# Prologue of a hybrid layer: scaling moved to VectorE, the first pair's sums placed behind x1's pieces, the output weights copied later

## The chip, the core and the metric

The program runs on one core of a Trainium2 chip. The metric is the device time of one execution in microseconds; lower is better. The engines are TensorE (PE in the profile; PEld is its weight load), VectorE (DVE), ScalarE (ACT), GpSimd (POOL) and SyncE (SP), which issues most DMAs. Each engine works through its own list of instructions in order and waits on semaphores.

## The reference

One decoder layer over 1024 tokens of width 1024, all in float32: RMSNorm, one wide projection, a Mamba-2 branch and a forgetting-attention branch beside each other, a gated merge, an output projection and a second RMSNorm. Only its start matters here:

```python
h = _rmsnorm(x, pre_g)                       # x * rsqrt(mean(x^2) + eps) * pre_g
proj = jnp.einsum('bld,de->ble', h, w_in)    # -> z_ssm, xBC, dt, q, k, v, f, z_att, g_ssm, g_att
...
out  = merged @ w_out
return x + _rmsnorm(out, post_g)
```

## The kernel before

**Products in seven steps.** Every wide product runs as a Strassen-like scheme on 2x2 blocks: seven block products instead of eight, each on a combination of blocks. The moving side is h turned (features on partitions), cut into blocks b11, b21 (first 512 tokens) and b22 and combinations t1, t2, t3, t4 (which need the other 512 tokens). Each operand is kept as a high piece and a low piece, both float32r; the tiles are `x0h`/`x0l` (b11), `x1h`/`x1l` (b21), `x2` (-b22), `x3` (t1), `x4` (-t2), `x5` (t3) and `x6` (t4), with four slices each. ScalarE writes the high piece and VectorE subtracts it to get the low one (`put`, L1211 to L1218). Step 1 uses x0, step 2 uses x1, step 6 uses x4, step 5 uses x3, step 7 uses x5, step 4 x6 and step 3 x2. One step is 12 matmuls of 128x512 in two halves.

**Weights.** A `Pair` of projection columns has four raw weight tiles (`raw`, six buffers, loaded on SP's queue). A step's weights (`wop`) are split in the same way, ScalarE first (L349), VectorE behind it (L350). Steps 6, 5, 7 and 3 take sums of raw tiles, made by `total` (L355) and in `prepare` (L371). `Stream` runs the steps of all pairs in a fixed list; `ahead` prepares the step that is three places further on when a step begins. The list begins with step 1 of the first pair, step 1 of the second, step 2 of each, then steps 6, 5, 7, 4 and 3 of the first pair.

**The prologue.** Eight tiles of x, 128 tokens each, are loaded (`xt`, L1187). `norm_tiles` takes the sum of squares, the root and the reciprocal, and scales the tile: tiles 0 to 3 on VectorE (L1201), 4 to 7 on GpSimd (L1203). TensorE turns slices of four tiles into PSUM (`pt`, two buffers, L1208); the copy out of PSUM multiplies by the norm's weight and makes `low` (L1228 on ScalarE, L1230 on VectorE). For k = 0 to 7 that gives the slices of x0 and x1; from k = 4 on, half a step of the stream runs behind each. Then come four rounds (j = 0 to 3): the other tokens' two slices are turned and copied (`up` and `b`, L1248), eight matmuls into `df` follow, VectorE makes `th` (L1254, L1257), their pieces x3 and x4, and the differences in `low` (L1262, L1263), and half a step runs. Behind the rounds stand the pieces of x5, x6 and x2 while steps 6, 5 and 7 of the first pair run.

**Output weights.** Twelve DMAs copy w_out from the input into `wo_dram` (L1237), 256 KB each. Nothing in the prologue reads it.

**Order.** Matmuls, turns and the operations under `pin` keep the program's order; a scheduler places the others. DMAs of the SP and ACT queues are given eight counters in turn, and a DMA is issued only when the DMA before it on its counter has landed. The short-lived tiles `th`, `up`-differences, gates and outputs share four buffers (`small`, L136); the first gate that is computed (`th` of the first pair, L415) goes through a tanh (L629) and is stored from such a buffer to `gs_dram` on ScalarE's queue (L630).

## Time and profile before

| | |
|---|---|
| median of 3 runs | 1278.63 us (1276.34 to 1283.66) |
| profiled execution, whole | 1273.87 us |
| its span, first to last instruction | 1272.2 us |
| PE, DVE, ACT, POOL busy | 1246.1, 1012.9, 794.3, 319.3 us |
| first step of the stream begins | 18.19 us |
| VectorE finishes the fourth round's last piece of x4 | 48.12 us |
| `summing` (L1304), first work behind the prologue's products | 59.01 us |

The profile lists, by engine, when an instruction began and how long it took; a bracket gives the idle time of its engine in front of it and what ended that. Instructions on one engine overlap a little, so a group's time is less than its count times the time of one.

### The profile page before, as it was taken

What the parts mean: (1) busy time and instruction counts of PE and PEld (TensorE: products, weight loads), DVE (VectorE), ACT (ScalarE), POOL (GpSimd) and SP (SyncE); (2) the same over time, 40 slices, a digit from 0 to 9 for tenths busy, and PEclk for the clock granted to TensorE, in tenths of its full rate; (3) what the DMA queues carried; (4) which work ended last, traced back from release to release, by engine and by line L of the source; (5) the groups of instructions that cost most, each with busy time, mean ns of one, the idle gap of its engine ahead of it and who ended that gap; (6) DMA issues with size and microseconds to landing.
All of it is one profiled execution on the core that took longest, in us unless ns stands there. A gap on an engine that the chain in (4) does not pass through costs nothing.

```text
span 1272.2 us, 20822 instructions
## 1 busy us (share of the span) xinstructions
PE 1246.1 (98%) x6926; PEld 982.3 (77%) x6926; DVE 1012.9 (80%) x1994; ACT 794.3 (62%) x1737; POOL 319.3 (25%) x322
## 2 busy tenths in 40 slices
PE   5999999999999999999999999999999999999997
PEld 3678888888888888888887777777777777778886
DVE  7988886988888978997767676767789767886975
ACT  7745665556665765566555666666687666844753
POOL 4000440013400241115102124223112212356062
PEclk9999999999999999999999999999999999999999
DMA  8232452545436533744447576666687657766933
GB/s 300 69 120 76 146 162 88 191 152 182 138 101 215 175 127 117 219 146 140 142 149 252 162 228 212 217 214 218 232 286 263 224 184 249 249 221 199 364 110 105
DMA packets 152236, 233.56 MB, mean 184 GB/s; under 512 B 15201, under 2 KB 60737, under 8 KB 152129
## 3 DMA queue, kind: packets, MB, share of 16 engines
q1 hardware_dynamic: 136064, 196.08, 47.7%
q10 hardware_dynamic: 10560, 18.06, 3.8%
q0 software_dynamic: 5504, 18.09, 3.7%
q8 instruction: 54, 0.88, 0.3%
q14 instruction: 54, 0.43, 0.1%
HBM read 162.99 MB, written 72.34 MB: 185 GB/s over the span
## 4 chain that ended last, share of the span: by engine, by line
PE 86%; DMA 4%; DVE 4%; ACT 4%; issue 1%; SPq 0%; POOL 0%; DVEq 0%; ACTq 0%; POOLq 0%
PE pb L128 36%; PE pc L128 21%; PE pd L128 7%; PE av L128 5%; PE pt L131 5%; PE s L128 5%; PE yps L128 2%; PE st L128 1%; ACT ex L1509 1%; DMA xt<-in_x 1%; PE tr L131 1%; PE tr_v L131 1%; DMA v<-v_dram 1%; PE df L128 1%; DVE wop L350 1%
## 5 line engine op out<-in xcount | busy, mean ns | idle before, releaser
L350 DVE TENSOR_TENSOR wop<-sum,wop 128x512 fp32r<-128x512 f32 x180 | 140.2, 780 | 53.6 <-ACT wop L349 52.6
L349 ACT ACTIVATE wop<-sum 128x512 fp32r<-128x512 f32 x180 | 112.5, 626 | 109.0 <-DVE sum L355 52.4
L1509 ACT ACTIVATE ex<-ex,nm 128x512 f32<-128x512 f32 (+1 forms) x192 | 116.2, 606 | 71.9 <-DVE nm L1505 71.6
L402 ACT ACTIVATE s<-pb 128x512 f32<-128x512 f32 x144 | 85.3, 593 | 98.2 <-PE pb L128 96.2
L128 PE MATMUL pb<-x0h,wop 128*128 128x512 f32 x384 | 131.5, 399 | 0.0
L128 PE MATMUL pb<-x6h,wop 128*128 128x512 f32 x384 | 129.5, 395 | 1.3 <-ACT s L402 1.3
L128 PE MATMUL pb<-x5h,wop 128*128 128x512 f32 x384 | 130.1, 396 | 0.7 <-ACT s L402 0.7
L350 DVE TENSOR_TENSOR wop<-raw,wop 128x512 fp32r<-128x512 f32 x144 | 105.4, 733 | 31.8 <-ACT wop L349 31.5
L128 PE MATMUL pc<-x3h,wop 128*128 128x512 f32 x384 | 129.8, 396 | 0.5 <-DVE ot L419 0.4
L128 PE MATMUL pc<-x2h,wop 128*128 128x512 f32 x384 | 130.2, 397 | 0.0
L128 PE MATMUL pb<-x4h,wop 128*128 128x512 f32 x384 | 129.1, 395 | 0.0
L1505 DVE CUSTOM_DVE_ANT_0 ex<-s,fb 128x512 f32<-128x512 f32 (+1 forms) x192 | 96.8, 552 | 20.0 <-PE s L128 14.8
L349 ACT ACTIVATE wop<-raw 128x512 fp32r<-128x512 f32 x144 | 89.7, 623 | 14.7 <-PE pd L128 6.1
L128 PE MATMUL pd<-x1h,wop 128*128 128x512 f32 x288 | 96.3, 394 | 0.0
L128 PEld LDWEIGHTS pb<-x6h,wop 128*128 128x128 f32 x384 | 72.1, 188 | 18.6 <-issue 2.0
L128 PEld LDWEIGHTS pb<-x5h,wop 128*128 128x128 f32 x384 | 72.1, 188 | 18.4 <-issue 2.0
L128 PEld LDWEIGHTS pb<-x0h,wop 128*128 128x128 f32 x384 | 72.6, 189 | 17.6 <-issue 2.9
L128 PEld LDWEIGHTS pc<-x3h,wop 128*128 128x128 f32 x384 | 72.1, 188 | 17.7 <-issue 1.5
L128 PEld LDWEIGHTS pc<-x2h,wop 128*128 128x128 f32 x384 | 72.1, 188 | 17.4 <-issue 2.4
L128 PEld LDWEIGHTS pb<-x4h,wop 128*128 128x128 f32 x384 | 72.1, 188 | 16.7 <-issue 1.9
L211 POOL TENSOR_TENSOR wd<-wd 128x256 f32<-128x256 f32 x32 | 32.4, 1011 | 205.0 <-DMA wd<-in_wo 135.0
L131 PE MATMUL pt<-ident,ex 128*128 128x128 f32 x576 | 75.1, 273 | 2.0 <-ACT ex L1509 1.4
(318 smaller groups left out, 2993.6 us busy)
## 6 DMA issues: line engine op xcount, KB each, us to landing
raw<-in_wu SPq DMA_DIRECT2D x128, 256.0 KB
csb<-cs_dram SPq DMA_DIRECT2D x32, 256.0 KB
q<-q_dram SPq DMA_DIRECT2D x32, 256.0 KB
k<-k_dram SPq DMA_DIRECT2D x16, 512.0 KB
fb<-f_dram SPq DMA_DIRECT2D x16, 512.0 KB
rb<-st_dram SPq DMA_DIRECT2D x48, 128.0 KB
wd<-in_wo SPq DMA_DIRECT2D x40, 128.0 KB
xt<-in_x SPq DMA_DIRECT2D x8, 512.0 KB
```

Source lines behind the costliest of these rows:

```text
L128: return tc.keep_in_program_order(nc.tensor.matmul(*args, **kw))
L131: return tc.keep_in_program_order(nc.tensor.transpose(out_, in_, idn))
L211: pin(nc.gpsimd.tensor_tensor(t[out_], t[a_], t[b_], ALU.subtract))
L349: nc.scalar.activation(op[:, 0], src, AF.Copy)
L350: nc.vector.tensor_tensor(op[:, 1], src, op[:, 0], ALU.subtract)
L402: nc.scalar.activation(s, ps, AF.Copy)
L1505: nc.vector.tensor_tensor_reduce(o, s[e][:, 0:w], fb[hp, h][:, e, 0:w], 1.0, 3.0e38, ALU.add, ALU.min, nm)
L1509: pin(nc.scalar.activation(o, o, AF.Exp, scale=-1.0, bias=nm, accum_out=hd.at(hd.sm, i, h, e)))
```

## The change

Four things are changed, and every one lies in the prologue.

1. `norm_tiles` scales all eight tiles of x on VectorE. The four scalings of tiles 4 to 7 are placed behind the low piece of x0's last slice (`held`).
2. The copies of turned slices k = 2 and 3 are made by VectorE, as k = 0 and 1 were; ScalarE keeps k = 4 to 7.
3. The first pair's sums in `total` are placed behind the last low piece of x1 (`behind`), and `ahead` prepares nothing when the second step begins, and two steps (places 4 and 5 of the list: steps 6 and 5 of the first pair) when the third begins.
4. The twelve copies into `wo_dram` are issued behind all steps of the prologue instead of behind `norm_tiles`.

```diff
         def total(self, x, y):
             t = wp.tile([P, KH, P], F32, tag="sum", bufs=2, name="sum")
-            self.adds.tensor_tensor(t, x, y, ALU.add)
+            with tc.issue_after(self.behind) if self.behind else nullcontext():
+                self.adds.tensor_tensor(t, x, y, ALU.add)
             return t
...
         def ahead(self, after):
-            if self.at + 3 < len(self.steps):
-                p, which = self.steps[self.at + 3]
+            for n in {1: (), 2: (4, 5)}.get(self.at, (self.at + 3,)):
+                if n >= len(self.steps):
+                    return
+                p, which = self.steps[n]
                 if after == (p.keys[0][0] == "merged"):
                     self.prepare(p, which)
...
-                if hf == 0:
+                with tc.issue_after(behind) if behind else nullcontext():
                     nc.vector.tensor_scalar(xt, xt, rstd[:, t : t + 1], None, ALU.mult)
-                else:
-                    nc.gpsimd.tensor_scalar(xt, xt, rstd[:, t : t + 1], None, ALU.mult)
...
-            if k > 1:
+            if k >= KH:
                 nc.scalar.activation(low[:, k, :], pt, AF.Copy, scale=preg[:, k : k + 1])
             else:
                 nc.vector.tensor_scalar(low[:, k, :], pt, preg[:, k : k + 1], None, ALU.mult)
-            put("b11" if k < KH else "b21", k % KH, low[:, k, :])
+            made = put("b11" if k < KH else "b21", k % KH, low[:, k, :])
+            stream.pairs[0].behind = made[1]
+            if k == KH - 1:
+                held = made[1]
             if k >= KH:
                 stream.halves(1)
-        norm_tiles(1, tiles2)
-
-        for k, h in [(k, h) for j in range(KH) for k, h in ((j, 0), (j + KH, 0), (j + KH, 1))]:
-            pin(nc.sync.dma_start(wo_dram[k, :, half(h)], a["wo"][k * P : (k + 1) * P, half(h)]))
+        norm_tiles(1, tiles2, held)
...
         stream.halves(5)
+        for k, h in [(k, h) for j in range(KH) for k, h in ((j, 0), (j + KH, 0), (j + KH, 1))]:
+            pin(nc.sync.dma_start(wo_dram[k, :, half(h)], a["wo"][k * P : (k + 1) * P, half(h)]))
```

TensorE's instructions stand in the same order as before, and behind the start so do those of every engine: the differences lie in the first 160 or so instructions of VectorE's list (to about 85 us in the profile before), the first 100 of ScalarE's, the first 30 of SP's, and in GpSimd's four scalings, which are gone. The lines of the new program are four to six higher (L1201 is L1205, L355 is L357, L350 is L351).

VectorE between x0's last low pieces and the first round, before. `wop<-raw` are the weights of the next three steps, `sum` and `wop<-sum` the first pair's sums for steps 6, 5 and 7, and `th<-up,low` is the first operation of round j = 0:

```order
L1215 TENSOR_TENSOR x0l<-low,x0h 128x512 x2
L350 TENSOR_TENSOR wop<-raw,wop 128x512 x2
L1199 RECIPROCAL rstd<-rstd 128x1
L350 TENSOR_TENSOR wop<-raw,wop 128x512
L1215 TENSOR_TENSOR x1l<-low,x1h 128x512
L350 TENSOR_TENSOR wop<-sum,wop 128x512
L1215 TENSOR_TENSOR x1l<-low,x1h 128x512
L371 TENSOR_TENSOR sum<-sum,raw 128x512
L1215 TENSOR_TENSOR x1l<-low,x1h 128x512 x2
L350 TENSOR_TENSOR wop<-sum,wop 128x512
L355 TENSOR_TENSOR sum<-raw 128x512
L1254 TENSOR_TENSOR th<-up,low 128x512
```

The same place now:

```order
L1217 TENSOR_TENSOR x0l<-low,x0h 128x512
L1205 TENSOR_SCALAR xt<-xt,rstd 128x1024 x3
L1203 RECIPROCAL rstd<-rstd 128x1
L351 TENSOR_TENSOR wop<-raw,wop 128x512 x2
L1217 TENSOR_TENSOR x1l<-low,x1h 128x512
L351 TENSOR_TENSOR wop<-raw,wop 128x512
L1205 TENSOR_SCALAR xt<-xt,rstd 128x1024
L1217 TENSOR_TENSOR x1l<-low,x1h 128x512 x3
L357 TENSOR_TENSOR sum<-raw 128x512
L1256 TENSOR_TENSOR th<-up,low 128x512
L357 TENSOR_TENSOR sum<-sum,raw 128x512
```

Three scalings of whole tiles stand ahead of the weights of the second pair's step 1, and the sums with the operations behind them (two `sum`, two `wop<-sum`, L373 and the sum for step 7) have moved in among the rounds.

VectorE behind the prologue, before. `th<-s,pc` (L419) empties the PSUM bank `pc` of the first pair, which the second pair's step 5 fills next; the `sum<-raw` behind it waits for two weight tiles that are loaded into the buffers which the operations on the third and on the fifth of these rows leave free:

```order
L350 TENSOR_TENSOR wop<-sum,wop 128x512
L1306 TENSOR_SCALAR cst<-cst 128x80
L371 TENSOR_TENSOR sum<-sum,raw 128x512
L687 COPY t<-pt_df 128x128 x2
L355 TENSOR_TENSOR sum<-raw 128x512
L692 SCALAR_TENSOR_TENSOR t<-t 128x256
L350 TENSOR_TENSOR wop<-sum,wop 128x512
L419 TENSOR_TENSOR th<-s,pc 128x512
L695 TENSOR_SCALAR t<-t 128x256
L350 TENSOR_TENSOR wop<-raw,wop 128x512
L355 TENSOR_TENSOR sum<-raw 128x512
L696 RECIPROCAL t<-t 128x256
```

The same place now:

```order
L351 TENSOR_TENSOR wop<-sum,wop 128x512
L373 TENSOR_TENSOR sum<-sum,raw 128x512
L357 TENSOR_TENSOR sum<-raw 128x512
L691 COPY t<-pt_df 128x128 x2
L696 SCALAR_TENSOR_TENSOR t<-t 128x256
L351 TENSOR_TENSOR wop<-sum,wop 128x512
L699 TENSOR_SCALAR t<-t 128x256
L700 RECIPROCAL t<-t 128x256
L357 TENSOR_TENSOR sum<-raw 128x512
L421 TENSOR_TENSOR th<-s,pc 128x512
L351 TENSOR_TENSOR wop<-raw,wop 128x512
```

The reciprocal and the sum that waits for loads have moved ahead of the operation that empties `pc`.

SP's queue, before:

```order
L342 DMA raw<-in_wu 128x512 x4
L1237 DMA wo_dram<-in_wo 128x512 x12
L342 DMA raw<-in_wu 128x512 x2
L663 DMA q_dram<-th 128x512
L342 DMA raw<-in_wu 128x512 x2
```

And now:

```order
L343 DMA raw<-in_wu 128x512 x6
L1284 DMA wo_dram<-in_wo 128x512 x12
L667 DMA q_dram<-th 128x512
L343 DMA raw<-in_wu 128x512 x2
L1300 DMA cst<-in_cst 128x128
```

The copies stand behind the second pair's last two weight tiles and ahead of the first store to `q_dram`; SP waits for nothing but their counters, so it issues them as soon as those two loads are out.

More of the change, by code (lines that the diff above doesn't have):

```diff
@@ L333, in __init__ @@
             self.s1, self.sums = None, 0
+            self.behind = None
         def load(self, names):
@@ L1189, in load_tiles, with norm_tiles @@
             return tiles
-        def norm_tiles(hf, tiles):
+        def norm_tiles(hf, tiles, behind=None):
             for t, xt in enumerate(tiles, 4 * hf):
```

## The prediction

> **What bounds the kernel now.** The page of the profile comes first: the busy time of the engines and the chain of work that ended last.

> ```profile
> PE 1246.1 (98%) x6926; PEld 982.3 (77%) x6926; DVE 1012.9 (80%) x1994; ACT 794.3 (62%) x1737; POOL 319.3 (25%) x322
> PE 86%; DMA 4%; DVE 4%; ACT 4%; issue 1%; SPq 0%; POOL 0%; DVEq 0%; ACTq 0%; POOLq 0%
> ```

> TensorE makes 86% of the chain and is hardly ever idle, so what the change is worth is the TensorE idle time that it takes away or adds in the prologue. The view of busy time by stage shows how much there is (columns: time, PE, PEld, DVE, ACT, POOL, granted clock, DMA share, GB/s):

> ```profile
> 10.00:20.00 10.00, 6.34 (x22) 4.77 (x23) 8.21 (x16) 8.80 (x19) 5.80 (x2) 1.00 1.04 401
> 20.00:30.00 10.00, 9.31 (x49) 6.13 (x47) 9.56 (x15) 9.49 (x19) 7.09 (x3) 1.00 0.74 242
> 30.00:40.00 10.00, 10.00 (x50) 5.26 (x47) 9.30 (x16) 7.07 (x11) 0.00 (x0) 1.00 0.10 29
> 40.00:50.00 10.00, 9.70 (x46) 6.40 (x45) 9.08 (x16) 7.85 (x15) 0.00 (x0) 1.00 0.10 37
> 50.00:60.00 10.00, 8.16 (x39) 6.23 (x37) 10.00 (x21) 7.84 (x16) 0.83 (x2) 1.00 0.29 101
> 60.00:70.00 10.00, 10.00 (x46) 8.30 (x46) 8.53 (x17) 4.45 (x9) 0.62 (x1) 1.00 0.47 159
> ```

> From 10 to 60 us TensorE is idle for 3.66 + 0.69 + 0 + 0.30 + 1.84 = 6.49 us. That is the most that this change could bring, 0.5% of 1273.87 us, and it would have to remove every gap. VectorE is nearly full from 20 us on, and wholly full from 50 to 60. The chain in order of time agrees: TensorE from 28.97, VectorE from 45.62, TensorE again from 60.33.

> ```profile
> 28.97 1.62 PE df L128 x6
> 45.62 0.69 DVE th L415
> 60.33 2.80 PE pc L128 x12
> ```

> So the prologue ends when VectorE is through its list, and the change gives VectorE more to do.

> **The head, to 30 us.** The timeline has the rows that matter:

> ```profile
> 14.20 12.89 POOL L1203 TENSOR_SCALAR xt<-xt,rstd 128x1024 f32<-128x1024 f32 x4 [12.83 <-DVE rstd L1199]
> 15.66 1.04 ACT L1197 ACTIVATE sqt<-xt 128x1024 bf16<-128x1024 f32 x1
> 17.42 1.11 PE L131 MATMUL pt<-ident,xt 128*128 128x128 f32 x4 [1.37 <-ACT low L1228]
> 17.80 1.41 DVE L355 TENSOR_TENSOR sum<-sum,raw 128x512 f32<-128x512 f32 x1
> 24.00 0.63 ACT L349 ACTIVATE wop<-sum 128x512 fp32r<-128x512 f32 x1
> 25.04 1.26 ACT L1228 ACTIVATE low<-pt,preg 128x512 f32<-128x512 f32 x2
> 27.14 0.76 PE L131 MATMUL pt<-ident,xt 128*128 128x128 f32 x5 [0.60 <-POOL xt L1203]
> 49.24 1.89 DVE L1215 TENSOR_TENSOR x5l<-low,x5h 128x512 fp32r<-128x512 f32 x3
> 8.52 0.75 DVE L1201 TENSOR_SCALAR xt<-xt,rstd 128x1024 f32<-128x1024 f32 x1
> ```

> Two waits of TensorE go: 1.37 us for ScalarE's copy of slice 2, which VectorE now makes at once, and 0.60 us for GpSimd. ScalarE loses two copies of 0.58 us (1.15 us, the two of the 25.04 row without their overlap of 0.1) and, to later, two `wop<-sum` of 0.52 us (0.63 less 0.1): 2.2 us before the first `up`. VectorE loses the sums ahead of 30 us and the slowing beside GpSimd (1.41 us for a sum that takes 0.69 elsewhere), and gains four scalings. One of these costs 0.67 us and a half-width operation 0.60 us when rows follow each other (0.75 less the overlap; 1.89 us for three).

> What is late next is ScalarE's high piece of x0's last slice. Behind the 15.66 row ScalarE has that square (1.04), a piece (0.52), a square (1.05), a root (0.18) and a copy (0.58), then the piece: its end is at 15.66 + 3.37 + 0.63 = 19.66. VectorE's low piece starts at 19.7 (0.6), the three scalings behind it take 2.0, and the low weights of the second pair's step 1 are ready 0.7 us later, at about 23.0. So TensorE keeps only part of its 2 us: I take 1.0 us gained at 30 us, between 0.6 (the POOL wait alone) and 2.0.

> **The rounds and the store.** From 19.7 VectorE has no gap. Up to the operation that empties `pd` it has four scalings (2.7 with a reciprocal) and 22 half-width operations (13.2), so it gets there at 35.6; before it was 36.69. Behind it runs a chain that the old trace shows whole:

> ```profile
> 36.69 0.69 DVE L415 TENSOR_TENSOR th<-pd,s 128x512 f32<-128x512 f32 x1 [0.49 <-PE pd L128]
> 38.50 1.28 ACT L629 ACT_TABLE_LOAD   x1
> 39.71 0.69 DVE L355 TENSOR_TENSOR sum<-raw 128x512 f32<-128x512 f32 x1
> 40.45 0.35 ACTq L630 DMA_DIRECT2D gs_dram<-th  x1
> 41.00:42.00 1.00, 1.00 (x10) 0.83 (x9) 0.48 (x1) 0.85 (x2) 0.00 (x0) 1.00 0.66 258
> 42.73 0.69 DVE L1254 TENSOR_TENSOR th<-up,low 128x512 f32<-128x512 f32 x1
> 47.43 0.69 DVE L1217 SCALAR_TENSOR_TENSOR x4l<-th,x4h 128x512 fp32r<-128x512 f32 x1
> 48.17 0.50 PE L128 MATMUL pb<-x4l,wop 128*128 128x512 f32 x1 [0.30 <-DVE x4l L1217]
> 12.00 10.54 SPq L1237 DMA_DIRECT2D wo_dram<-in_wo  x12
> 51.76 0.33 SPq L663 DMA_DIRECT2D q_dram<-th  x1
> ```

> The last round's `th` (42.73) takes the buffer that the gate's store reads; the DMAs move that store from 41 to 42 us, when they have nothing else. In the new order ScalarE has two more operations ahead of the table load (a `wop<-sum` and a piece of x4, 1.04 us), which eat the 1.0 us gained: the store again leaves at about 40.5. But the wo copies are now under way. SP issues them behind the loads into the two buffers that the first pair's sums free, at about 35.5; seven can go before a counter stops SP, and at 10.54 / 12 = 0.88 us each they last from about 37.5 (behind the two loads) to 43.7. The store meets some three of them.

> Its landing is bounded by 42.4 (nothing lost) and 45.0 (served behind all seven); I take 43.3, which is its 1 us of transfer at half rate, since the 41.00 row has it alone at 258 GB/s. VectorE, there at about 41, waits until then: 43.3 instead of 42.73 is +0.6. Behind it stands one operation more than before, the second pair's sum (before at 39.71, ahead of it), +0.6. The last piece of x4, which TensorE waited for already, comes 1.2 us later: +1.2 us (from 0.3 to 2.9). The head's gain is swallowed in this wait. From there to `summing` both orders hold the same 18 half-width operations, so the 1.2 us stay.

> [...]

> **Behind the prologue.** VectorE's rows there:

> ```profile
> 59.01 0.16 DVE L1304 TENSOR_TENSOR summing<-ident 128x64 f32<-128x64 f32 x1
> 61.59 0.68 DVE L355 TENSOR_TENSOR sum<-raw 128x512 f32<-128x512 f32 x1
> 63.58 0.68 DVE L419 TENSOR_TENSOR th<-s,pc 128x512 f32<-128x512 f32 x1
> 65.69 0.39 PE L128 MATMUL pc<-x3h,wop 128*128 128x512 f32 x1
> 66.10 0.69 DVE L355 TENSOR_TENSOR sum<-raw 128x512 f32<-128x512 f32 x1 [1.03 <-DMA raw<-in_wu]
> 66.71 1.75 DVE L696 RECIPROCAL t<-t 128x256 f32<-128x256 f32 x1
> ```

> Before, `pc` was emptied at 63.58 and VectorE waited for its weight tiles afterwards, which cost TensorE nothing. Now the reciprocal and the sum that waits for the load stand in front of that operation. Counted from `summing`, at S: two `wop`, a constant, two sums end at S + 2.9; the load, issued then, takes 66.10 - (61.59 + 0.69) = 3.8 us as before; the sum 0.6 and the emptying 0.7 end at S + 8.0. TensorE wants the bank at S + 65.69 - 59.01 = S + 6.7: it waits 1.3 us. Were the load quick, the reciprocal (1.66 us, begun near S + 4.4) would still hold the emptying until S + 7.3: 0.6 us. I take 1.2, nearer to the load's own row.

> The rest is free or out of reach: the wo copies leave the time from 12 us on, where the x tiles and raw tiles that matter stood ahead of them on the same queue, so no load there becomes earlier; and SP, held at the eighth copy until the store has landed (43.3), has issued the rest by about 46, ahead of the next DMA on its queue (51.76).

> **Sum.** 1.2 + 1.2 = +2.4 us on the profiled execution, 1273.87 to 1276.3. That execution lies 4.8 us below the median of the three runs; on the median the forecast is 1278.63 + 2.4 = 1281.0 us.

> **The rivals.** *The head's gain is kept*: the store lands at 42.4 or VectorE has the buffer by another way, x4's last piece comes 1.0 us earlier, and only the wait for `pc` is left: from -1.0 to +0.3, 1277.6 to 1278.9. For it speaks that TensorE waited only 0.30 us for x4; against it that VectorE has no idle time from 20 us on to draw on. *The store is served behind all copies*: +2.9 + 1.3 = +4.2, 1282.8. For it speaks that all DMAs share one set of engines, against it that two queues are at work. [...] *Slower by over 0.5%* (6.4 us; about what a measurement of this kernel can tell from no change): the same wait on the buffer, decided by the copies' pace. The term must reach 5.2, so the store must land at 47.3; that takes 1.4 us per copy in place of 0.88. The old copies kept to 0.88 while the DMAs moved 401 and then 242 GB/s, more than there is to move now. *Faster by over 0.5%* needs all 6.49 us of idle time gone and no new wait. That the change does nothing is excluded by the order.

> **How the numbers follow.** Forecast 0.54; head kept 0.22; behind all copies 0.15; slower by over 0.5% 0.06; faster by over 0.5% 0.03. Within 0.5%: 0.54 + 0.22 + 0.15 = 0.91. The runs shown lie up to 2.3 below and 5.0 above their median. The range goes from the head kept in full, less some two thirds of the one (1277.6 - 1.6), to the store behind all copies, plus about half of the other (1282.8 + 2.7): 1276.0 to 1285.5.

> **What would show it.** Right: TensorE waits neither at 17.4 nor at 27.1; the last round's `th` (L1256) begins after 43 us with VectorE idle for the store in front of it; `pb<-x4l` comes after 49 us; `summing` begins near 60.2; and TensorE waits about 1 us for L421 ahead of `pc<-x3h` near 68. Wrong: `summing` before 59, or no idle time of TensorE between 60 and 70 us.

## The result, and the profile after

Over 20 runs each, the median went from 1277.87 us to 1284.58 us: ratio 1.0052, 95% interval 1.0042 to 1.0061. A second set of 5 runs of the changed kernel gave 1281.42 against 1276.70 us, 1.0036 (1.0024 to 1.0048). The change costs 0.36 to 0.52%, where 0.19% (+2.4 us) was forecast; 1281.0 had been forecast for the median and 1276.0 to 1285.5 as its range. The profiled execution took 1284.84 us (span 1283.1).

Page of the changed kernel, busy time and the shares of the chain:

```profile
PE 1251.2 (98%) x6926; PEld 984.9 (77%) x6926; DVE 1015.9 (79%) x2000; ACT 793.6 (62%) x1735; POOL 303.4 (24%) x318
PE 79%; DVE 8%; DMA 5%; ACT 4%; issue 3%; SPq 1%; POOL 0%; DVEq 0%; ACTq 0%; POOLq 0%
```

TensorE still sets the end, but VectorE and the DMAs now hold 13% of the chain instead of 8%. Busy time by stage (columns as in the prediction):

```profile
10.00:20.00 10.00, 7.73 (x31) 5.92 (x31) 8.07 (x17) 8.98 (x20) 0.00 (x0) 1.00 0.75 301
20.00:30.00 10.00, 9.05 (x46) 5.92 (x45) 10.00 (x18) 9.12 (x17) 0.00 (x0) 1.00 0.01 2
30.00:40.00 10.00, 9.96 (x49) 5.17 (x48) 10.00 (x18) 6.57 (x11) 0.00 (x0) 1.00 0.41 125
40.00:50.00 10.00, 7.20 (x30) 3.85 (x29) 4.82 (x9) 3.77 (x7) 0.00 (x0) 0.96 0.63 201
50.00:60.00 10.00, 9.01 (x29) 6.35 (x27) 10.00 (x17) 8.99 (x17) 0.00 (x0) 0.69 0.56 180
70.00:80.00 10.00, 7.90 (x28) 6.07 (x28) 6.73 (x15) 2.51 (x5) 0.00 (x0) 0.83 0.22 75
```

From 10 to 20 us TensorE gained 1.4 us of work, as meant. From 40 to 50 it is idle for 2.8 us and VectorE for 5.2, while the DMAs carry five times what they carried before (201 for 37 GB/s). From 50 to 60 and from 70 to 80 us the granted clock, 1.00 in all of these stages before, is 0.69 and 0.83. The timeline shows both places:

```profile
34.46 0.87 SPq L343 DMA_DIRECT2D raw<-in_wu  x2
35.38 13.86 SPq L1284 DMA_DIRECT2D wo_dram<-in_wo  x12
...
46.27 0.69 DVE L1256 TENSOR_TENSOR th<-up,low 128x512 f32<-128x512 f32 x1 [4.27 <-DMA gs_dram<-th]
49.42 0.79 PE L128 MATMUL pb<-x4l,wop 128*128 128x512 f32 x1 [2.69 <-DVE x4l L1219]
52.42 0.79 PE L128 MATMUL pb<-x4l,wop 128*128 128x512 f32 x1 [0.95 <-DVE x4l L1219]
63.27 0.16 DVE L1308 TENSOR_TENSOR summing<-ident 128x64 f32<-128x64 f32 x1
67.90 1.75 DVE L700 RECIPROCAL t<-t 128x256 f32<-128x256 f32 x1
71.09 0.69 DVE L357 TENSOR_TENSOR sum<-raw 128x512 f32<-128x512 f32 x1 [1.43 <-DMA raw<-in_wu]
71.70 0.68 DVE L421 TENSOR_TENSOR th<-s,pc 128x512 f32<-128x512 f32 x1
72.52 0.47 PE L128 MATMUL pc<-x3h,wop 128*128 128x512 f32 x1 [2.10 <-DVE th L421]
76.36 0.51 PE L128 MATMUL pc<-x3l,wop 128*128 128x512 f32 x1
```

Two rows of the timeline before, to set beside these:

```profile
59.23 1.10 PE L128 MATMUL pt_df<-summing,dft 128*128 128x64 f32 x8 [0.53 <-DVE summing L1304]
67.96 0.39 PE L128 MATMUL pc<-x3l,wop 128*128 128x512 f32 x1
```

The changed kernel's chain in order of time has the first of the two places in two rows:

```profile
40.24 5.93 DMA gs_dram<-th
46.88 0.68 DVE sum L357
```

The gate's store, issued at 40.24 us, landed at 46.17. Before it was issued at 40.45 and VectorE used its buffer at 42.73. So the last round's `th` begins 3.54 us later, the second pair's sum behind it adds 0.6, and `summing` comes 4.26 us later (63.27 for 59.01). TensorE is 4.57 us behind at the last product ahead of `pc` (70.04 for 65.47), and the second wait adds 2.3: `pc<-x3h` comes 6.83 us later (72.52 for 65.69). The last step is the clock. The trace's record of it falls to 0.50 at 49.29 and 73.19 us and is back at 1.00 at 56.12 and 76.60; the windows are cut 0.13 to 0.15 us ahead of these changes:

```profile
45.74:49.15 3.41, 0.99 (x5) 0.48 (x3) 2.88 (x5) 0.68 (x2) 0.00 (x0) 1.00 0.43 131
49.16:55.97 6.81, 5.56 (x11) 3.60 (x12) 6.81 (x13) 5.97 (x12) 0.00 (x0) 0.51 0.57 166
69.64:73.04 3.40, 1.30 (x6) 0.81 (x5) 1.97 (x5) 1.74 (x3) 0.00 (x0) 1.00 0.28 105
73.06:76.45 3.39, 3.39 (x10) 2.63 (x9) 2.63 (x7) 0.00 (x0) 0.00 (x0) 0.52 0.45 146
76.46:79.87 3.41, 3.41 (x16) 2.84 (x15) 2.03 (x5) 0.63 (x1) 0.00 (x0) 0.98 0.02 8
```

After 3.41 us in which TensorE worked for 0.99 us (0.85 in the 3.41 us up to the fall itself), its clock was halved for 6.83 us; after 3.41 us with 1.30 us of work (1.31), for 3.41 us. At half clock a matmul takes 0.43 us instead of 0.23. The first stretch costs little, since TensorE waited behind it before, too: the product `pt_df`, which uses `summing`, begins 4.7 us later (63.89 for 59.23), `summing` itself 4.26. The second costs 1.6 us: the matmul at 76.36 stands 8.4 us behind its place before (67.96).

8.4 us between two traces is more than the medians differ. The profiled execution of before is faster than each of the 20 runs (1273.87, where their median is 1277.87), so traces compared with it show some 4 us too much over the whole run. Why the part up to 80 us, too, is larger in the traces than in the medians stays open. The sizes below are taken from the ratios, the places from the traces.

### The profile page after: what moved, and what is told of

Read it like the earlier page. It is cut to its first block, busy times and chain, and to the rows that moved or that the text cites. A ratio compares the mean times of both kernels' runs of the same rounds, so it can differ in the third digit from the quotient of the medians.

```text
span 1283.1 us, 20815 instructions
## 1 busy us (share of the span) xinstructions
PE 1251.2 (98%) x6926; PEld 984.9 (77%) x6926; DVE 1015.9 (79%) x2000; ACT 793.6 (62%) x1735; POOL 303.4 (24%) x318
## 4 chain that ended last, share of the span: by engine, by line
PE 79%; DVE 8%; DMA 5%; ACT 4%; issue 3%; SPq 1%; POOL 0%; DVEq 0%; ACTq 0%; POOLq 0%
PE pb L128 33%; PE pc L128 20%; PE pd L128 6%; PE av L128 5%; PE s L128 5%; PE pt L131 5%; PE yps L128 2%; DVE wop L351 2%; DMA raw<-in_wu 1%; DVE sum L357 1%; DMA xt<-in_x 1%; PE st L128 1%; ACT ex L1513 1%; PE tr L131 1%; PE tr_v L131 1%
## 5 line engine op out<-in xcount | busy, mean ns | idle before, releaser
L351 DVE TENSOR_TENSOR wop<-sum,wop 128x512 fp32r<-128x512 f32 x180 | 140.9, 784 | 55.2 <-ACT wop L350 54.1
L350 ACT ACTIVATE wop<-sum 128x512 fp32r<-128x512 f32 x180 | 112.4, 626 | 107.3 <-DVE sum L357 48.5
L128 PE MATMUL pc<-x3h,wop 128*128 128x512 f32 x384 | 132.0, 402 | 2.6 <-DVE th L421 2.1
L128 PE MATMUL pb<-x0h,wop 128*128 128x512 f32 x384 | 131.5, 399 | 0.9 <-DVE wop L351 0.9
L128 PE MATMUL pb<-x5h,wop 128*128 128x512 f32 x384 | 129.9, 395 | 0.8 <-ACT s L404 0.7
L351 DVE TENSOR_TENSOR wop<-raw,wop 128x512 fp32r<-128x512 f32 x144 | 105.3, 732 | 31.6 <-ACT wop L350 31.3
L128 PE MATMUL pb<-x4h,wop 128*128 128x512 f32 x384 | 130.2, 397 | 0.0
L128 PE MATMUL pc<-x2h,wop 128*128 128x512 f32 x384 | 130.2, 397 | 0.0
L128 PE MATMUL pb<-x6h,wop 128*128 128x512 f32 x384 | 129.5, 395 | 0.7 <-ACT s L404 0.7
L350 ACT ACTIVATE wop<-raw 128x512 fp32r<-128x512 f32 x144 | 89.6, 623 | 15.2 <-PE pd L128 6.8
L128 PE MATMUL pd<-x1h,wop 128*128 128x512 f32 x288 | 96.3, 394 | 0.0
L128 PEld LDWEIGHTS pc<-x3h,wop 128*128 128x128 f32 x384 | 73.5, 191 | 20.8 <-ACT wop L350 2.5
L128 PEld LDWEIGHTS pb<-x0h,wop 128*128 128x128 f32 x384 | 72.5, 189 | 18.8 <-issue 2.9
L128 PEld LDWEIGHTS pb<-x5h,wop 128*128 128x128 f32 x384 | 72.1, 188 | 18.4 <-issue 2.0
L128 PEld LDWEIGHTS pb<-x6h,wop 128*128 128x128 f32 x384 | 72.1, 188 | 17.9 <-issue 2.0
L128 PEld LDWEIGHTS pb<-x4h,wop 128*128 128x128 f32 x384 | 72.5, 189 | 17.4 <-issue 1.9
L128 PEld LDWEIGHTS pc<-x2h,wop 128*128 128x128 f32 x384 | 72.1, 188 | 17.2 <-issue 2.4
L128 PE MATMUL pb<-x4l,wop 128*128 128x512 f32 x192 | 75.7, 394 | 3.6 <-DVE x4l L1219 3.6
```

The lines of the kernel that those rows point to most:

```text
L128: return tc.keep_in_program_order(nc.tensor.matmul(*args, **kw))
L350: nc.scalar.activation(op[:, 0], src, AF.Copy)
L351: nc.vector.tensor_tensor(op[:, 1], src, op[:, 0], ALU.subtract)
```

## The experiments

Ratios are to the kernel before on the same chip, with 95% intervals.

**The copies back at their old place.** The changed kernel with its fourth part undone:

```diff
         norm_tiles(1, tiles2, held)
+        for k, h in [...]:
+            pin(nc.sync.dma_start(wo_dram[k, :, half(h)], ...))
...
         stream.halves(5)
-        for k, h in [...]:
-            pin(nc.sync.dma_start(wo_dram[k, :, half(h)], ...))
```

> The changed kernel with the twelve wo copies issued at their old place, the other parts kept. Theory 1 (the gate's store lands at 46 us because the copies are under way, and VectorE's th waits for its buffer): the store lands by 42.5 us, VectorE no longer stands idle for 4.3 us ahead of L1256's last operation, pb<-x4l comes before 47.5 us and the clock stays at 1.00 from 40 to 60 us. The wait for pc near 68 us, which is another matter, stays at about 2 us. Time: 1284.6 - 4.3 = 1280.3, between 1279 and 1281.5, so +1 to +3.5 over before. Theory 2 (the store is late for what VectorE and ScalarE now do, the copies only stand beside it): still over 1283, store landing after 45 us.

Measured: 1.0021 (1.0008 to 1.0034), 1278.90 us. Timeline of this kernel:

```profile
42.75 0.69 DVE L1259 TENSOR_TENSOR th<-up,low 128x512 f32<-128x512 f32 x1 [0.34 <-DMA gs_dram<-th]
48.91 0.50 PE L128 MATMUL pb<-x4l,wop 128*128 128x512 f32 x1 [1.12 <-DVE x4l L1219]
68.53 0.47 PE L128 MATMUL pc<-x3h,wop 128*128 128x512 f32 x1 [1.92 <-DVE th L421]
```

The 4.27 us are now 0.34, and 1.5 to 3.1 thousandths (2 to 4 us) of the loss are gone: the copies delay the store. `pb<-x4l` came at 48.9, not before 47.5 as expected, since the second pair's sum stands behind the wait here too. The 1.92 us for `pc` stay, as they should.

**A buffer of its own for the store.** Copies and store go out as in the changed kernel; only the tile that the first gate's store reads is nobody else's:

```diff
+    first = [lambda: pro.tile([P, HALF], F32, name="th")]
...
         def dst(ch):
-            t[ch] = small()
+            t[ch] = first.pop()() if first else small()
```

> The changed kernel, with the tile of the first gate's store in a buffer that nothing else uses; store and copies go out as before. Theory 1 (the loss is the reuse of the store's buffer by the last round's th): the store still lands at 45 to 46.5 us, but VectorE does not wait for it, the last x4l is ready by 49 us and the clock stays at 1.00 from 40 to 60 us; the wait for pc stays. The ratio to before falls from the changed kernel's 1.0052 to that with the copies at their old place, 1.0021 (1.0008 to 1.0035). Theory 2 (the crowded DMA engines are the loss, through other loads that come late): 1.0045 or more, the idle time of VectorE only ending on another transfer.

Measured: 1.0019 (1.0009 to 1.0030), 1278.16 us.

```profile
40.56 0.35 ACTq L636 DMA_DIRECT2D gs_dram<-th  x1
42.23 0.68 DVE L1258 TENSOR_TENSOR th<-up,low 128x512 f32<-128x512 f32 x1
48.38 0.50 PE L128 MATMUL pb<-x4l,wop 128*128 128x512 f32 x1 [0.68 <-DVE x4l L1221]
68.46 0.53 PE L128 MATMUL pc<-x3h,wop 128*128 128x512 f32 x1 [2.38 <-DVE th L421]
```

The store left into DMAs as busy as in the changed kernel (205 GB/s from 40 to 50 us, for 201 there and 37 before), yet `th` ran at 42.23 without a wait, 1.67 us after the issue, where the store of before took 2.01 us to land with nothing beside it (40.45 to 42.46). The ratio is that of the copies at their old place. Busy DMAs by themselves cost nothing that the ratio shows: the loss is the reuse of the buffer. Two edits that have nothing else in common agree on its size. Both intervals lie below that of the first set (1.0042 to 1.0061); with that of the second (1.0024 to 1.0048) they overlap, so the size is less sure than the wait.

**The copies alone.** The kernel before, with only the fourth part of the change (the lines of the first diff, moved the other way).

> The kernel before with only the wo copies moved behind the prologue. Theory 1 (copies delay the store, store holds the buffer): store lands at 45 to 46.5 us, VectorE idle 3 to 4 us ahead of the last round's th, pb<-x4l 3 to 4.5 us later than before, clock 0.5 for some 7 us after it, no wait of TensorE for the operation that empties pc. Time +3 to +5 over before, 1281 to 1283. Theory 2 (copies harmless by themselves): within 1 us of before, th at about 42.7 us.

Measured: 0.9997 (0.9988 to 1.0005), 1276.00 us. The loss that theory 1 expected did not come. Timeline of this kernel:

```profile
30.07 15.36 SPq L1279 DMA_DIRECT2D wo_dram<-in_wo  x12
40.33 0.35 ACTq L630 DMA_DIRECT2D gs_dram<-th  x1
42.60 0.69 DVE L1251 TENSOR_TENSOR th<-up,low 128x512 f32<-128x512 f32 x1
48.05 0.50 PE L128 MATMUL pb<-x4l,wop 128*128 128x512 f32 x1 [0.32 <-DVE x4l L1217]
```

Here SP begins with the copies at 30.07 us, not 35.38. The seven that its counters let out are through at about 40 us (an estimate: from 30 to 40 us the DMAs moved 213 GB/s, 2.1 MB, which is what the load ahead of the copies and seven of them hold), and VectorE does not wait for the store issued at 40.33. What puts the copies onto the store is the third part of the change: the first pair's sums come later, so the two raw buffers that they free come later, and SP holds the two loads into them, with the copies behind, until 34.5 us.

**The sums back.** The changed kernel without its third part:

```diff
-            for n in {1: (), 2: (4, 5)}.get(self.at, (self.at + 3,)):
+            for n in (self.at + 3,):
...
-            stream.pairs[0].behind = made[1]
```

> The changed kernel with the first pair's sums free of the wait on x1's pieces and the weights of steps 4 and 5 made at their old steps; scaling, copies of turned tiles and moved wo copies stay. Theory 1 (two separate losses): on VectorE th<-s,pc stands ahead of the reciprocal and of the sum that waits for its load again, so TensorE waits under 0.3 us for pc<-x3h and the clock stays 1.00 from 60 to 80 us; the wait for the store stays, with pb<-x4l after 48.5 us. Time 1284.6 - 2.2 (wait) - 1.6 (matmuls at half clock) = 1280.8, between 1279.8 and 1282. Theory 2 (the second loss follows from the first, by the shift in time): pc<-x3h still waits about 2 us and the time stays over 1283.5.

Measured: 1.0009 (0.9999 to 1.0019), 1277.13 us. The order at `pc` and the clock came out as expected, but the wait for the store went too, for the reason just given (the copies begin at 31.04 us here), and 1.0009 stands where the expected 1280.8 us would have been about 1.0023:

```profile
31.04 14.80 SPq L1283 DMA_DIRECT2D wo_dram<-in_wo  x12
42.63 0.69 DVE L1255 TENSOR_TENSOR th<-up,low 128x512 f32<-128x512 f32 x1
48.44 0.50 PE L128 MATMUL pb<-x4l,wop 128*128 128x512 f32 x1 [0.30 <-DVE x4l L1219]
```

**Scaling and copies of turned tiles alone.** Both of the diffs above together, so that the first two parts of the change are left.

> Only the scaling of all tiles by VectorE and its two more copies of turned tiles are left of the change; sums and wo copies as before. Theory 1 (both losses come from the other two parts): no idle time of VectorE for the store, no wait for pc, clock 1.00 throughout to 100 us, the 1.0 to 1.7 us won by 30 us kept wholly or in part: -1.5 to +0.3 against before, 1276.4 to 1278.2. Theory 2 (VectorE, given more to do, is late by itself): +1 or more, 1279 or over, with summing after 60 us.

Measured: 1.0003 (0.9992 to 1.0014), 1277.27 us. TensorE's 1.1 us won at 17 us are gone by 23.5, and `summing`'s product stands at 59.76 us for 59.23. These parts do nothing that can be measured, either way.

**The later sums, without and with the copies.** The kernel before with only the third part, and with the third and fourth.

> The kernel before with one part of the change: the first pair's sums behind x1's pieces and the weights of steps 4 and 5 made together. Theory 1 (without the moved copies nothing collides, and without the scaling on VectorE the order at pc stays): no wait of VectorE for the store, pc<-x3h at once, ratio 0.9990 to 1.0010. Theory 2 (the later sums cost by themselves, since both kernels with this part and without either wait measured 1.0018 to 1.0021): 1.0012 to 1.0022, with TensorE's waits for the second pair's weights or for x4.

> The kernel before with two parts of the change: the later sums and the moved wo copies. Theory 1 (the later sums hold the two raw loads on SP's queue, the copies behind them fall onto the store): copies begin at 32 to 34 us instead of 30, seven of them end near 41 to 43 us; the store, issued near 40.5, lands at 42.5 to 44 us, VectorE waits 0 to 2 us, ratio 1.0005 to 1.0025. Theory 2 (the two parts only collide with VectorE's scaling in front): ratio as with the later sums alone, store landed by 42.5 us.

Measured: 1.0013 (1.0003 to 1.0023) and 1.0018 (1.0009 to 1.0028). The timeline with the third part alone:

```profile
29.20 1.15 ACT L350 ACTIVATE wop<-sum 128x512 fp32r<-128x512 f32 x2 [1.02 <-DVE sum L357]
30.98 1.05 PE L128 MATMUL df<-b,wdf 128*32 128x512 f32 x2 [1.69 <-ACT b L1255]
```

and with both:

```profile
34.29 14.68 SPq L1286 DMA_DIRECT2D wo_dram<-in_wo  x12
43.87 0.35 ACTq L634 DMA_DIRECT2D gs_dram<-th  x1
45.99 0.69 DVE L1258 TENSOR_TENSOR th<-up,low 128x512 f32<-128x512 f32 x1 [0.36 <-DMA gs_dram<-th]
```

The later sums cost by themselves: ScalarE waits 1.02 us for them, the copy of `b` behind it is late, and TensorE waits 1.69 us. With the copies moved as well, they do go out as late as in the changed kernel, but the whole chain of the gate is later too; the store leaves at 43.87, when the seven copies are nearly through (at about 44.4 us, an estimate from the 10.2 us that they took in the changed kernel from the first issue to the last landing), and VectorE waits for it 0.36 us only, to 45.99. The ratio came out as expected, the wait by another way. By these traces the collision needs the later sums, the moved copies and the head made shorter by the first two parts.

**The order at pc.** The changed kernel, the third pair's first sum behind the operation that empties `pc`; and the same with the copies at their old place:

```diff
+            behind = stream.pairs[0].gave if self is stream.pairs[2] else self.behind
-            with tc.issue_after(self.behind) if self.behind else nullcontext():
+            with tc.issue_after(behind) if behind else nullcontext():
...
-                    nc.vector.tensor_tensor(d, s, ps, ALU.subtract)
+                    self.gave = nc.vector.tensor_tensor(d, s, ps, ALU.subtract).ins
```

> The changed kernel, with one more ordering: the third pair's first sum, which waits for its load, stands behind the operation that empties pc. Theory 1 (the two losses add up, the second is the order at pc): pc<-x3h waits under 0.3 us, the clock is 1.00 from 70 to 80 us, and the ratio falls from 1.0052 by 2 to 4 us to 1.0020 to 1.0037; the wait for the store stays as it was. Theory 2 (VectorE is late with pc anyway, for the reciprocal in front of it): the wait shrinks to some 1 us and the ratio falls by 1 us at most, to 1.0044 or more.

> The changed kernel with the wo copies at their old place and the third pair's first sum behind the operation that empties pc: both losses taken away, all else of the change kept. Theory 1 (they are all that the change costs): no wait of over 1.3 us of TensorE between 17 and 90 us, clock 1.00, ratio 0.9990 to 1.0006. Theory 2 (the later sums cost VectorE and TensorE something of their own): 1.0010 or more, with TensorE's waits elsewhere.

Measured: 1.0046 (1.0034 to 1.0058) and 1.0018 (1.0009 to 1.0027). The busy time by stage of the first, and a row of its timeline:

```profile
70.00:80.00 10.00, 10.00 (x46) 8.29 (x45) 8.90 (x20) 4.25 (x8) 0.00 (x0) 1.00 0.28 105
```

```profile
70.41 0.63 DVE L422 TENSOR_TENSOR th<-s,pc 128x512 f32<-128x512 f32 x1
```

TensorE has no idle time from 70 to 80 us and the clock stays at 1.00: the mechanism is as described. But the ratios hardly move: 1.0046 lies between the changed kernel's two values, and 1.0018 beside 1.0021, and both are in the bands of theory 2. The wait for `pc`, 1.8 to 2.4 us long in the traces, is worth too little to be told from nothing here, at most some 2 us. And with both waits gone 1.0018 is left (the trace has 1.1 us of wait for `x4l` and 0.2 for `pc`): the later sums cost something of their own. Why the first ratio did not fall, the traces show in part, below.

**Nine useless matmuls.** The changed kernel, with matmuls into a bank that nobody reads in front of the product that waits for `pc`:

```diff
             xh, xl = self.ops[x]
+            if which == 5 and self is stream.pairs[1]:
+                idle = pp.tile([P, HALF], F32, tag="tr", bufs=2, name="idle")
+                for _ in range(9):
+                    mm(idle, op[:, 0, 0, :], xh[:, 0, :], start=True, stop=True)
```

> The changed kernel with nine matmuls more, of the second pair's step-5 operands into a bank of their own that nobody reads, just ahead of the matmuls that wait for pc: 9 x 0.23 = 2.0 us, about as long as the wait. Theory 1 (TensorE's idle time brings the granted clock down for the 3.4 us that follow, at a price of 1.6 us of its own): the clock stays at 1.00 from 70 to 80 us, twelve pc<-x3 matmuls take 2.8 us and not 4.6, and the ratio falls from 1.0052 by 1 to 1.7 us, to 1.0039 to 1.0044, though more is computed. Theory 2 (the low clock has another cause, or is made up for later): ratio 1.0050 to 1.0058.

Measured: 1.0055 (1.0042 to 1.0068), 1282.65 us. Timeline:

```profile
71.33 2.20 PE L128 MATMUL idle<-x3h,wop 128*128 128x512 f32 x9
73.37 0.39 PE L128 MATMUL pc<-x3h,wop 128*128 128x512 f32 x1
76.09 0.39 PE L128 MATMUL pb<-x5h,wop 128*128 128x512 f32 x1
```

In the trace theory 1 holds: the clock stays at 1.00 from 60 to 80 us, and the twelve matmuls of `pc` take 2.72 us (73.37 to 76.09) instead of 4.42 (72.52 to 76.94). The ratio lies in the band of theory 2. So it was the idle time that brought the clock down there (0.83 from 70 to 80 us with it, 1.00 with TensorE busy), but what this one stretch costs is under what 5 runs can tell.

The traces of the four kernels side by side say more. The first two columns are how much later than before TensorE began `pt_df` (59.23 before) and the second pair's first `pb<-x5h`, behind the products of `pc` (68.42 before); the last is the ratio, in us of before.

| kernel | `pt_df` | `pb<-x5h` | from the ratio |
|---|---|---|---|
| changed, first trace | 4.7 | 8.5 | 6.6 |
| changed, second trace (below) | 4.0 | 7.6 | 4.6 |
| order at `pc` | 6.4 | 6.3 | 5.9 |
| nine useless matmuls | 5.7 | 7.7 | 7.0 |

Between the two places the changed kernel loses 3.9 and 3.6 us, the new order nothing and the useless matmuls 2.0: both edits save there about what was expected. But in their traces the store came later, and the last round's `th` with it (47.11 us with the new order and 46.93 with the useless matmuls, for 46.27 and 45.92), and the half clock behind it delayed `pt_df` by 1.3 and 0.8 us more than `summing`, for 0.4 and 0.1. So they had lost more by `pt_df`, which eats about half of the saving or more.

```profile
47.11 0.69 DVE L1257 TENSOR_TENSOR th<-up,low 128x512 f32<-128x512 f32 x1 [4.55 <-DMA gs_dram<-th]
```

Whether the store is that late in all executions of these two kernels, one trace of each does not tell.

**The changed kernel again.**

> The changed kernel once more, for a second trace of it beside the others. Theory 1 (its two waits are fixed by the order): the same two waits as in its first trace, 4 us of VectorE for the store and 2 us of TensorE for pc, ratio 1.0042 to 1.0061; the half-clock stretches need not lie at the same places. Theory 2 (the late landing was a mishap of one execution): store landing by 44 us and a ratio under 1.0040 or over 1.0065.

Measured: 1.0036 (1.0024 to 1.0048), 1281.42 us. The ratio is in theory 2's band (under 1.0040), but the waits are those of theory 1:

```profile
45.92 0.69 DVE L1256 TENSOR_TENSOR th<-up,low 128x512 f32<-128x512 f32 x1 [3.70 <-DMA gs_dram<-th]
49.07 0.50 PE L128 MATMUL pb<-x4l,wop 128*128 128x512 f32 x1 [2.13 <-DVE x4l L1219]
71.61 0.47 PE L128 MATMUL pc<-x3h,wop 128*128 128x512 f32 x1 [1.83 <-DVE th L421]
```

The late landing is no mishap: 45.8 us for 46.2.

**A version meant to beat both.** The kernel before, with x0's four slices copied by VectorE and the first pair's sums held back only behind x0's low pieces, not x1's:

```diff
-            if k > 1:
+            if k >= KH:
                 nc.scalar.activation(low[:, k, :], pt, AF.Copy, ...)
...
+            if k < KH:
+                stream.pairs[0].behind = made[1]
```

> A version that might beat both: the kernel before with x0's four turned tiles copied by VectorE and the first pair's sums only behind x0's low pieces; GpSimd still scales the second half, wo copies at their old place. Theory 1 (TensorE's 1.37 us at 17.4 us can be kept when VectorE's list does not grow ahead of the second pair's low weights): 0.5 to 1 us less than before, ratio 0.9990 to 1.0000. Theory 2 (VectorE's two added copies, 1.2 us, come back as waits for x4 and x6, since VectorE sets the end of the prologue): 1.0000 to 1.0010, head gained and lost again by 60 us.

Measured: 0.9986 (0.9976 to 0.9996), 1275.36 us: 1.3 us under before, somewhat more than the 0.5 to 1 us of theory 1, and the only kernel here whose interval lies wholly below 1.

```profile
58.99 1.10 PE L128 MATMUL pt_df<-summing,dft 128*128 128x64 f32 x8 [0.56 <-DVE summing L1310]
```

The trace rather has what theory 2 says of the head. TensorE is ahead by up to 2.0 us near 17.6, part of it because its matmuls take 0.23 us there from 16.8 us on and those of before 0.43 until 20.0; from 42 us on it is ahead by 0.24 us only (58.99 for 59.23). That is less than the 1.3 us. So the gain in the ratio has no shown cause beyond 0.2 us, and one such interval among thirteen can be chance.

## Why the prediction was partly right

**The number.** The sum gave +2.4 us, and 4.7 and 6.7 us were measured. The median 1284.58 lies in the range because its upper end, 1285.5, was taken from the rival "served behind all copies" with half of the spread on top; that rival's own 1282.8 was passed, too. That the number fell inside is luck.

**Right in sign, place and structure.** TensorE waits neither at 17.4 nor at 27.1 us; the last round's `th` begins after 43 us with VectorE idle for the store; `pb<-x4l` comes after 49 us (the last piece's at 52.42); the 18 operations from there to `summing` pass the delay on unchanged (3.54 + 0.6 at `th`, 4.26 at `summing`); and the reciprocal and the sum ahead of L421 make TensorE wait for `pc`.

**The step that failed: where the store lands.** The prediction bounded it by 42.4 and 45.0 and took 43.3, "its 1 us of transfer at half rate". It landed at 46.17, past the upper bound. The seven copies ran from 38.1 to 45.5 us instead of 37.5 to 43.7, 1.06 us each and not 0.88, one of the 16 DMA engines about 0.9 us behind the others. The 0.88 was the pace at which SP had issued the old copies. Counted as the new ones, from the landing of the load ahead of them, the old twelve took 0.78 us each (18.3 to 27.6 us in the trace of before), so their pace did not carry over; in the kernel with the copies alone seven took about 1.1 us each, with no store beside them (an estimate: from 32.3 us, if the load issued at 29.69 takes the 2.6 us of before, to about 40). Why the pace fell is not shown. And the store did not pass any of them: the sixteen increments of the seventh copy's counter came from 43.1 to 45.5 us, those of the store's from 43.7 to 46.2, one behind the other by 0.6 us. Nor did the store's data move early: in the trace no packet of ScalarE's queue moved before 42.7 us, 2.5 us after the issue, where before all of them moved between 41.3 and 42.1, within 1.7 us of it. This is the rival "served behind all copies", given 0.15, with a higher price. What held data and increments back alike is not shown. The term, sized +1.2, measured +4.3 us at `summing` in the trace and 2 to 4 us in the ratios.

**The other term** was sized +1.2 and measured 2.1 us of wait: counted as in the prediction, the load took 4.9 us (66.20 to 71.09) instead of 3.8. In the time it is not to be told from nothing.

**The clock** was not in the prediction at all. Both waits halved it in the trace, at a price of at most 0.4 us for the first and of 1.6 for the second. It is no matter of one trace: 22 of the 25 runs of the changed kernel had a mean clock of 0.995 or 0.996, and none of the 86 runs of before beside the experiments had less than 0.997. Its size in the medians stays open.

**The later sums** were priced only through what they move (the order at `pc`, SP's queue). Alone they cost 1.0013. In the changed kernel's trace TensorE is ahead of before until 42.4 us (by 0.5), so that loss is not added there in the same form. But the three kernels with all but the wait for the store (0.35 us of it at most) measured 1.0018 to 1.0021, and the two with early sums and VectorE's scaling 1.0003 to 1.0009.

**"Slower by over 0.5%"**, given 0.06, asked for a store that lands at 47.3 us. It landed at 46.2, and 1.0052 still reached the limit, by the clock and the second wait; the second set, 1.0036, did not.

## What to carry to other kernels

When a bulk transfer is moved, ask what holds it on its queue now: here a reordering of sums on VectorE, not the move itself, set the copies five microseconds later and onto a store. A store from a shared buffer is a promise to the next user of the buffer; price it by the landing behind everything then in flight (here 5.9 us after the issue behind the copies of another queue, 2.0 us with nothing in flight), and give it a buffer of its own if the next user is on the chain. On a part where one engine is full and the change gives it more, look first at what it does too early: holding two sums back by a few operations, with two copies added, was the only version that measured faster than before (and its trace accounts for a fifth of that), and moving whole jobs between engines won nothing that could be measured.
